# A decoder-layer step on one core: the late modulation steps write their transfers one place ahead of their matmuls

## The chip, the cores and the metric

One core of one Trainium2 chip runs the whole program. The metric is the device time of one execution in microseconds (us), as the median of several runs. Engines are named as the profile names them: PE (TensorE, the matmuls) and PEld (its weight loads), DVE (VectorE), ACT (ScalarE), POOL (GpSimd) and SP (SyncE, which here issues nearly all transfers; SPq is its queue).

## What is computed

One layer of a conditioned decoder in float32, for a 256-token prompt and for 8 sequences of 4 new tokens, so 288 columns in all. The conditioning vectors give six modulation vectors of 2048 values for each sequence; the rest is a gated-delta branch and a pooling branch that are merged, and then a feed-forward layer.

```python
mod = jax.nn.silu(c) @ w_ada + b_ada                       # w_ada: 2048 x 12288
sh1, sc1, gt1, sh2, sc2, gt2 = jnp.split(mod, 6, axis=-1)
u = ada_modulate(rms_norm(x, norm1_g), sh1, sc1)
mix, ... = token_mixers(u, ...)                            # u @ w_in, conv, delta rule, pooling, w_proj_a, w_proj_b, w_out
x = x + gt1[:, None, :] * mix
h = ada_modulate(rms_norm(x, norm2_g), sh2, sc2)
gate, up = jnp.split(h @ w_gate_up, 2, axis=-1)
x = x + gt2[:, None, :] * ((jax.nn.silu(gate) * up) @ w_down)
```

## The kernel before

**Weight chunks.** Every large product runs through `gemm` (L127 to L147). It takes a panel of 512 output columns and walks over its rows in chunks of 256 (`KB = 2` blocks of 128). For each chunk, `load_raw` (L114) has SP load a tile `raw` of 512 KB, ACT rounds each half into `wh` (L123), DVE (in a few panels POOL) subtracts to get the rest `wl` (L124), and PE does 24 matmuls of 128x288 (L141), six for each of the four output tiles `g0` to `g3`. There are `RAW = 7` tiles `raw` and `WH = 4` each of `wh` and `wl`, which are two chunks' worth. When a panel is done, `evac` empties `g0` to `g3`, in some panels with DVE's addition to `acc` (L435).

**Modulation steps.** The generator `ada` (L181 to L232) computes one modulation vector and gives control back after each step. Its late calls, the vectors `M_GT1`, `M_SC2`, `M_SH2` (the chain `later`) and `M_GT2` (`last_ada`), have `m == 16` and take 8 steps each. One step loads four tiles `raw` of 512 KB from `w_ada` and does 8 matmuls of 32x512 into `ada` (L218), which the profile records as 16. These four tiles come from the same seven `raw` tiles as the weight chunks, except the first two steps of `last_ada` (`ahead=2`), which load ahead into other tiles. After the last step the vector is turned round by PE (L225) and added up (L231).

**Where a step is written.** `gemm` calls `fill()` after each chunk; `Fill` adds `every` to a counter and resumes the generator each time the counter passes 1. `every` is 0.2 while `later` runs (one step in 5 chunks), and 0.085 for `last_ada` in the feed-forward layer (one in 11.8 chunks).

**What sets the order.** A scheduler that follows data, free tiles and priorities by its own clock puts what is written into one fixed order for each engine. `high_priority()` lets instructions go ahead; all matmuls of a step but the first have it. `issue_after(ins)` forbids that an instruction stands ahead of `ins` on its engine. Each engine then works strictly in its order, and SP too: a transfer that waits for a free `raw` tile holds back all transfers behind it.

Of the kernel before, what the change touches and what calls it, by code (L numbers as in the profile page):

```python
# [24 lines left out]
KB = 2  # L25
# [48 lines left out]
def tile_step(ctx: ExitStack, tc: tile.TileContext, at, t):  # L74
# [52 lines left out]
    def gemm(srcs_of, xs, evac, kbs, eng=vec, late=False):  # L127


        ps = [psg.tile([P, 512], F32, tag="g", name=f"g{j}") for j in range(4)]  # L130
        kbs = list(kbs)
        for c in range(0, len(kbs), KB):
            wh, wl = load_split(srcs_of(kbs[c]), eng)
            for j in range(4):
                o = ps[j][:, 0:N]
                last = c + KB == len(kbs)
                terms = [(w, x, i) for i in range(KB) for w, x in ((wh, 0), (wh, 1), (wl, 0))]
                if late and c == 0:
                    terms.sort(key=lambda v: v[1])
                for n, (w, x, i) in enumerate(terms):  # L140
                    mm = pe.matmul(o, w[i][:, j * P:(j + 1) * P], xs(kbs[c + i])[x], start=c + n == 0,  # L141
                                   stop=last and n == 3 * KB - 1)
                if last:
                    with tc.high_priority():
                        evac(j, o)
            fill()
        return mm  # L147

# [32 lines left out]
    def ada(*d0s, n=16, pool=None, ahead=0):  # L181


        m = n * len(d0s)
        w = m // 4 * P
        ps = psd.tile([P, 512], F32, tag="ada", name="ada")
        per = max(m // 8, 1)
        step = max(8 // m, 1)
        first = pool and d0s[0] == M_SH1
        pair = {4: 1 if first else 2, 8: 4, 16: 2}[m]  # L190

        def load(c, pool):
            loads = []
            for k in range(c, c + step * pair, step):
                raws = []
                for x in range(per):
                    if per > 1:
                        d = (d0s if len(d0s) > 1 else (d0s[0], d0s[0] + 8))[x]
                        srcs = [(t["w_ada"][0, k * P:(k + 1) * P, d * P:(d + 8) * P], 0, 1024)]
                    else:  # L200
                        srcs = [(t["w_ada"][0, k * P:(k + step) * P, d0 * P:(d0 + n) * P], i * n * P, (i + 1) * n * P)
                                for i, d0 in enumerate(d0s)]
                    raws.append(load_raw(srcs, qp if first and k >= 8 else pool, step))
                loads.append((k, raws))
            return loads

        early = {}
        for c in range(0, ahead * step * pair, step * pair):
            early[c] = load(c, pool or qp)
            yield  # L210
        for c in range(0, 16, step * pair):
            loads = early.get(c) or load(c, pool)

            todo = [(k, raws, i, j) for k, raws in reversed(loads) for i in range(step) for j in (2, 3, 0, 1)]
            for y, (k, raws, i, j) in enumerate(todo):
                x, q = divmod(j, 4 // per)
                with tc.high_priority() if y else nullcontext():
                    in_turn(pe.matmul(ps[32 * j:32 * j + 32, 0:w], cpad[:, k + i, :], raws[x][:, i, q * w:(q + 1) * w],  # L218
                                      start=c == 0 and y < 4, stop=c + step * pair == 16 and y + 4 >= len(todo)))
            if c + step * pair < 16:  # L220
                yield
        sb = wpool.tile([P, 512], F32, tag="adasb", name="adasb", bufs=1)
        act.copy(sb[:, 0:w], ps[:, 0:w])
        for i in range(0, w, P):
            pe.transpose(ps[:, i:i + P], sb[:, i:i + P], ident)  # L225
        pv = ps[:, 0:w].rearrange("p (b q m) -> p q b m", q=4, m=32)
        k = 4 // len(d0s)
        for i, d0 in enumerate(d0s):
            md = mod[:, d0:d0 + n, :].rearrange("p (q b) m -> p q b m", q=k)
            v = va[:, d0:d0 + n].rearrange("p (q b) -> p q b", q=k)  # L230
            vec.tensor_tensor(md, pv[:, i * k:(i + 1) * k, :, 0:9], bc(v, 3, [P, k, n // k, 9]), ALU.add)  # L231
        yield  # L232
# [8 lines left out]

    class Fill:

        gen, every, n = iter(()), 1.0, 0.0

        def __call__(self):
            self.n += self.every
# [4 lines left out]
    fill = Fill()  # L252
# [65 lines left out]
    with tc.tile_pool(name="st", bufs=1) as st:  # L318
# [44 lines left out]
        for i in range(3):  # L363
            n = xt[i].shape[0]
# [22 lines left out]
        for n, (k0, k1) in enumerate(STEPS):  # L387
            dn = k1 - k0
# [36 lines left out]

            more = n + 1 < len(STEPS)
            fill.gen = first_ada(*STEPS[n + 1], st) if more else later
            fill.every = 4 / (dn // KB * len(FIRST) - 5) if more else 0.2
            for p, c0 in enumerate(FIRST):
                def evac(j, ps, n=n, p=p):  # L430
                    a = acc[p][:, j, :]
                    if n == 0:
                        act.copy(a, ps)
                    else:
                        vec.tensor_tensor(a, a, ps, ALU.add)  # L435
# [601 lines left out]
        mm = gemm(cols_of(t["w_out"][0], 512 * p), xs_m, evac, range(16))  # L1037
    with tc.issue_after(mm.ins):
        next(last_ada)
    fill.every, fill.n = 0.085, 0  # L1040


    rn = cst.tile([P, 3], F32, name="rn")
# [144 lines left out]
```

## Time and profile before

| what | value |
|---|---|
| median of 3 runs | 1805.72 us (1804.52 to 1808.49) |
| the profiled execution | 1801.66 us |
| its span, first to last instruction | 1799.8 us |
| PE busy | 1749.2 us, 97% |
| PEld busy | 1651.6 us, 92% |
| DVE / ACT / POOL busy | 1001.3 / 751.0 / 234.0 us |
| bytes moved | 371.23 MB, mean 206 GB/s |

The profiled execution is 1.86 us longer than its span and 4.06 us shorter than the median. Matmuls overlap in the records, so 97% does not mean that PE works at its peak; what counts is where PE waits, and for whom.

### The profile page before, as it was taken

To read this page: it belongs to the slowest core of one execution; us is meant where nothing else is said; L and a number is where in the kernel's file an instruction comes from. 1 tells how busy PE (TensorE), PEld (TensorE's weight loads), DVE (VectorE), ACT (ScalarE), POOL (GpSimd) and SP (SyncE) were. 2 spreads that over 40 slices of the span, in tenths; PEclk is the share of its full clock that TensorE was granted. 3 is DMA by queue.
4 is the path that set the end of the run, shared out by engine and by line. 5 is a ranking of instruction groups with operands and counts; after the bars stand their busy time and mean duration, and the time that the engine had idled before them with its cause. 6 is when DMAs were issued, how large, how long until landed. Compare 5 with 4: busy or idle time off the path is not lost.

```text
span 1799.8 us, 37784 instructions
## 1 busy us (share of the span) xinstructions
PE 1749.2 (97%) x14772; PEld 1651.6 (92%) x14772; DVE 1001.3 (56%) x2101; ACT 751.0 (42%) x1534; POOL 234.0 (13%) x391
## 2 busy tenths in 40 slices
PE   5999998999999999999999999999999999999997
PEld 3979997888899898899989999999999999999997
DVE  2456569755666676764564444455445445544454
ACT  4523346542344333444444444444334444444333
POOL 1000015420222444211241000000000000000000
PEclk9999999999999999999999999999999999999999
DMA  9988756677577585885647667665555555555542
GB/s 292 316 300 304 234 169 202 213 229 246 187 252 234 189 268 177 271 294 179 218 150 234 211 205 224 188 203 165 164 165 164 168 167 169 154 175 164 162 156 87
DMA packets 227210, 371.23 MB, mean 206 GB/s; under 512 B 18335, under 2 KB 118168, under 8 KB 226608
## 3 DMA queue, kind: packets, MB, share of 16 engines
q1 hardware_dynamic: 223224, 357.02, 61.7%
q0 software_dynamic: 3808, 11.80, 2.1%
q8 instruction: 116, 1.90, 0.4%
q14 instruction: 62, 0.51, 0.1%
HBM read 361.16 MB, written 7.96 MB: 205 GB/s over the span
## 4 chain that ended last, share of the span: by engine, by line
PE 91%; DMA 4%; DVE 2%; issue 1%; ACT 0%; POOL 0%; SPq 0%; DVEq 0%; POOLq 0%; ACTq 0%
PE g L141 81%; PE ada L218 4%; DMA raw<-in_w_ada_dram 3%; DVE wl L124 1%; PE pks L726 1%; DVE cy L286 0%; DMA raw<-in_w_in_dram 0%; PE py L646 0%; PE pp L651 0%; PE pnr L545 0%; PE py L907 0%; DMA xt<-in_x_prompt_dram 0%; PE px L1011 0%; DMA pw<-in_pool_w_dram 0%; DMA dtb<-in_dt_bias_dram 0%
## 5 line engine op out<-in xcount | busy, mean ns | idle before, releaser
L141 PE MATMUL g<-rq,wh 128*128 128x288 f32 x7296 | 1443.2, 298 | 10.6 <-DVE acc L435 6.2
L141 PEld LDWEIGHTS g<-rq,wh 128*128 128x128 f32 x7296 | 1150.8, 188 | 37.2 <-issue 10.9
L141 PE MATMUL g<-rq,wl 128*128 128x288 f32 x3648 | 1014.3, 296 | 0.3 <-POOL wl L124 0.3
L124 DVE TENSOR_TENSOR wl<-raw,wh 128x512 fp32r<-128x512 f32 x910 | 611.7, 702 | 627.0 <-ACT wh L123 606.7
L123 ACT CAST wh<-raw 128x512 fp32r<-128x512 f32 x944 | 545.3, 618 | 821.7 <-PE g L141 742.5
L141 PEld LDWEIGHTS g<-rq,wl 128*128 128x128 f32 x3648 | 664.8, 188 | 4.3 <-issue 1.3
L218 PE MATMUL ada<-raw,cpad 128*32 128x512 f32 (+2 forms) x1152 | 98.5, 474 | 16.0 <-DMA raw<-in_w_ada_dram 16.0
L169 POOL TENSOR_TENSOR ro<-ro,cfix 128x1 f32<-128x1 f32 (+1 forms) x3 | 1.6, 559 | 838.0 <-DVE ro L1150 838.0
L218 PEld LDWEIGHTS ada<-raw,cpad 128*32 128x32 f32 x1152 | 32.9, 115 | 52.8 <-issue 38.1
L435 DVE TENSOR_TENSOR acc<-acc,g 128x288 f32<-128x288 f32 x144 | 61.0, 448 | 23.3 <-PE g L141 23.0
L124 POOL TENSOR_TENSOR wl<-raw,wh 128x512 fp32r<-128x512 f32 x34 | 45.8, 1367 | 51.6 <-ACT wh L123 50.4
L141 PE MATMUL g<-q,wh 128*128 128x288 f32 x256 | 49.4, 294 | 0.0
L286 DVE SCALAR_TENSOR_TENSOR cy<-xc,vb,cy 128x312 f32<-128x312 f32 x72 | 42.5, 610 | 5.6 <-ACT cy L284 4.7
L141 PEld LDWEIGHTS g<-q,wh 128*128 128x128 f32 x256 | 40.3, 189 | 0.0
L141 PE MATMUL g<-q,wl 128*128 128x288 f32 x128 | 35.2, 296 | 0.0
L1099 DVE SCALAR_TENSOR_TENSOR fgg<-fth,fgg 128x288 f32<-128x288 f32 x44 | 20.0, 455 | 14.0 <-ACT fgg L1098 14.0
L973 DVE SCALAR_TENSOR_TENSOR x<-g,mod,x 128x256 f32<-128x256 f32 x48 | 22.9, 478 | 7.0 <-PE g L141 5.9
L1097 ACT ACTIVATE fth<-g 128x288 f32<-128x288 f32 x44 | 18.3, 416 | 13.5 <-PE g L141 13.4
L141 PEld LDWEIGHTS g<-q,wl 128*128 128x128 f32 x128 | 23.2, 188 | 0.0
L659 POOL MEMSET T<- 32x64 f32 x8 | 1.1, 155 | 156.7 <-PE pab L444 148.4
L1104 DVE TENSOR_TENSOR fgg<-fgg,g 128x288 f32<-128x288 f32 x44 | 19.9, 451 | 2.7 <-PE g L141 0.4
L1098 ACT ACTIVATE fgg<-g 128x288 f32<-128x288 f32 x44 | 18.4, 417 | 0.0
(336 smaller groups left out, 976.2 us busy)
## 6 DMA issues: line engine op xcount, KB each, us to landing
raw<-in_w_gate_up_dram SPq DMA_DIRECT2D x352, 256.0 KB, 2.9
raw<-in_w_in_dram SPq DMA_DIRECT2D x144, 512.0 KB, 4.6
raw<-in_w_ada_dram SPq DMA_DIRECT2D x128, 512.0 KB, 5.6
raw<-in_w_down_dram SPq DMA_DIRECT2D x88, 512.0 KB, 4.0
raw<-in_w_ada_dram SPq DMA_DIRECT2D x128, 256.0 KB, 5.5
raw<-in_w_out_dram SPq DMA_DIRECT2D x32, 512.0 KB, 3.9
raw<-in_w_proj_b_dram SPq DMA_DIRECT2D x16, 512.0 KB, 4.5
raw<-in_w_proj_a_dram SPq DMA_DIRECT2D x16, 512.0 KB, 4.6
```

The costliest lines, as they stand in the source:

```text
L123: act.copy(wh[i], raw[:, i, :])
L124: eng.tensor_tensor(wl[i], raw[:, i, :], wh[i].bitcast(F32), ALU.subtract)
L141: mm = pe.matmul(o, w[i][:, j * P:(j + 1) * P], xs(kbs[c + i])[x], start=c + n == 0, stop=last and n == 3 * KB - 1)
L218: in_turn(pe.matmul(ps[32 * j:32 * j + 32, 0:w], cpad[:, k + i, :], raws[x][:, i, q * w:(q + 1) * w], start=c == 0 and y < 4, stop=c + ste ...
L286: vec.scalar_tensor_tensor(y[:, 0:L], xc[:, m:m + L], vb[:, 24 * m + no:24 * m + no + 1], y[:, 0:L], ALU.mult, ALU.add)
L435: vec.tensor_tensor(a, a, ps, ALU.add)
L726: pe.matmul(pks[NS * i:NS * i + NS, x * P:(x + 1) * P], km[i // 2][:, i % 2, b, :], S[i][:, b, :], start=b == 0, stop=b == NB - 1)
L973: vec.scalar_tensor_tensor(x[:, j, 0:NP], ps[:, 0:NP], mod[:, gate + d, 0:1], x[:, j, 0:NP], ALU.mult, ALU.add)
L1097: act.activation(th, ps, AF.Tanh, scale=0.5)
L1098: act.activation(gg, ps, AF.Copy, scale=0.5)
L1099: vec.scalar_tensor_tensor(gg, th, 1.0, gg, ALU.add, ALU.mult)
L1104: vec.tensor_tensor(gg, gg, ps, ALU.mult)
```

## The change

In a late step (`m == 16`) the four loads are now written at one place between chunks and the matmuls at the next: the generator gives control back between the two. The first matmul of such a step may not stand ahead of the last matmul of the newest chunk, which `gemm` notes in `fill.last`. Steps whose loads were already written ahead (`ahead`) stay as they were. Since a step now needs two calls, `every` is doubled, to 0.4 and 0.17, so that a vector takes as many chunks as before. The 0.3 during the last panel of `w_out` stays.

```diff
                     with tc.high_priority():
                         evac(j, o)
+            fill.last = mm
             fill()
         return mm
...
             loads = early.get(c) or load(c, pool)
+            tied = m == 16 and c not in early
+            if tied:
+                yield
...
-                with tc.high_priority() if y else nullcontext():
+                with tc.high_priority() if y else tc.issue_after(fill.last.ins) if tied else nullcontext():
                     in_turn(pe.matmul(ps[32 * j:32 * j + 32, 0:w], cpad[:, k + i, :], raws[x][:, i, q * w:(q + 1) * w],
...
-        gen, every, n = iter(()), 1.0, 0.0
+        gen, every, n, last = iter(()), 1.0, 0.0, None
...
-            fill.every = 4 / (dn // KB * len(FIRST) - 5) if more else 0.2
+            fill.every = 4 / (dn // KB * len(FIRST) - 5) if more else 0.4
...
-    fill.every, fill.n = 0.085, 0
+    fill.every, fill.n = 0.17, 0
```

The queue of SP around the 14th late step, in the pooling branch, of before. Each row is a transfer into a `raw` tile; the names in brackets are the counters that it waits for: `DVE_49` and `PE_49` stand for work of DVE (a subtraction L124 that frees a `raw` tile) and of PE (a matmul of a step that frees one), `DMAHW` for transfers done long before.

```order
L114 DMA raw_7018<-in_w_in_dram 128x2x512 [waits DMAHW2_49,DVE_49]
L114 DMA raw_7163<-in_w_in_dram 128x2x512 [waits DMAHW3_49,DVE_49]
L114 DMA raw_7197<-in_w_in_dram 128x2x512 [waits DMAHW4_49,DVE_49]
L114 DMA raw_7231<-in_w_in_dram 128x2x512 [waits DMAHW1_49,DVE_49]
L114 DMA raw_7265<-in_w_in_dram 128x2x512 [waits DMAHW5_49,DMAHW0_49,PE_49]
L114 DMA raw_7299<-in_w_ada_dram 128x1024 [waits DMAHW7_49,DMAHW6_49,PE_49]
L114 DMA raw_7301<-in_w_ada_dram 128x1024 [waits PE_49]
L114 DMA raw_7303<-in_w_ada_dram 128x1024 [waits DMAHW2_49,DVE_49]
L114 DMA raw_7305<-in_w_ada_dram 128x1024 [waits PE_49]
L114 DMA raw_7315<-in_w_in_dram 128x2x512 [waits DMAHW3_49,DVE_49]
L114 DMA raw_7349<-in_w_in_dram 128x2x512 [waits DMAHW1_49,PE_49]
```

The same place in the changed kernel:

```order
L114 DMA raw_7018<-in_w_in_dram 128x2x512 [waits DMAHW2_49,DVE_49]
L114 DMA raw_7163<-in_w_in_dram 128x2x512 [waits DMAHW7_49,DVE_49]
L114 DMA raw_7197<-in_w_in_dram 128x2x512 [waits DMAHW3_49,DMAHW0_49,DVE_49]
L114 DMA raw_7231<-in_w_ada_dram 128x1024 [waits DMAHW4_49,DMAHW1_49,DVE_49]
L114 DMA raw_7233<-in_w_ada_dram 128x1024 [waits DMAHW6_49,DMAHW5_49,PE_49]
L114 DMA raw_7235<-in_w_ada_dram 128x1024 [waits PE_49]
L114 DMA raw_7237<-in_w_ada_dram 128x1024 [waits PE_49]
L114 DMA raw_7239<-in_w_in_dram 128x2x512 [waits DMAHW2_49,DVE_49]
L114 DMA raw_7273<-in_w_in_dram 128x2x512 [waits PE_49]
L114 DMA raw_7315<-in_w_in_dram 128x2x512 [waits DMAHW3_49,DVE_49]
L114 DMA raw_7349<-in_w_in_dram 128x2x512 [waits DMAHW0_49,DVE_49]
```

The four loads of the step moved ahead of two weight chunks in SP's queue: before, five chunks from `raw_7018` to `raw_7265` stand ahead of them, now three, and the other two stand behind. In both, three of the four loads wait for matmuls of the step before (`PE_49`).

PE's order at the matmuls of the same step, of before (`ada` is the step, `g1` to `g3` are output tiles of the chunk in work):

```order
L141 MATMUL g2_7161<-rq_263,wh_7200 128x288
L141 MATMUL g2_7161<-rq_264,wh_7200 128x288
L141 MATMUL g2_7161<-rq_263,wl_7202 128x288
L218 MATMUL ada_6121<-raw_7305,cpad_82 32x512 x2
L218 MATMUL ada_6121<-raw_7303,cpad_82 32x512 x2
L218 MATMUL ada_6121<-raw_7301,cpad_82 32x512 x2
L218 MATMUL ada_6121<-raw_7299,cpad_82 32x512 x2
L141 MATMUL g3_7162<-rq_263,wh_7165 128x288
L141 MATMUL g3_7162<-rq_264,wh_7165 128x288
```

And of the changed kernel:

```order
L141 MATMUL g3_7162<-rq_1352,wh_7276 128x288
L141 MATMUL g3_7162<-rq_1353,wh_7276 128x288
L141 MATMUL g3_7162<-rq_1352,wl_7278 128x288
L222 MATMUL ada_6053<-raw_7237,cpad_82 32x512 x2
L222 MATMUL ada_6053<-raw_7235,cpad_82 32x512 x2
L222 MATMUL ada_6053<-raw_7233,cpad_82 32x512 x2
L222 MATMUL ada_6053<-raw_7231,cpad_82 32x512 x2
L141 MATMUL g0_7159<-rq_2170,wh_7317 128x288
L141 MATMUL g0_7159<-rq_2171,wh_7317 128x288
```

The step moved from inside a chunk (60 chunk matmuls behind the step before it) to behind the chunk `raw_7273`, five whole chunks behind the step before it; `raw_7239` and `raw_7273` are the fourth and the fifth of these chunks.

## Rows read from the trace of the kernel before

**Rows 1.** The page: span, busy time of PE, granted clock and GB/s in 40 slices.

```profile
span 1799.8 us, 37784 instructions
PE 1749.2 (97%) x14772; PEld 1651.6 (92%) x14772; DVE 1001.3 (56%) x2101; ACT 751.0 (42%) x1534; POOL 234.0 (13%) x391
PEclk9999999999999999999999999999999999999999
...
GB/s 292 316 300 304 234 169 202 213 229 246 187 252 234 189 268 177 271 294 179 218 150 234 211 205 224 188 203 165 164 165 164 168 167 169 154 175 164 162 156 87
```

**Rows 2.** Whom PE waited for, 240 to 1180 us: total us, times, longest us.

```profile
PE g L141 <- DVE acc L435: 5.8, 4, 4.4
PE g L141 <- ACT rq L1070: 2.3, 1, 2.3
PE pn L986 <- DVE sq L1025: 1.8, 1, 1.8
PE ada L218 <- DMA raw<-in_w_ada_dram: 1.2, 2, 0.8
...
PE g L141 <- POOL wl L124: 0.3, 1, 0.3
```

**Rows 3.** Instructions of L218, 240 to 1180 us, and what their idle time waited for.

```profile
L218 PE MATMUL ada<-raw,cpad x512: 592/592/617, 263.4 to 1167.7; 128*32 128x512 f32 x171
its engine sat idle before it (us, times) until:
  issue: 23.4, 90
  DMA raw<-in_w_ada_dram: 3.2, 5
```

**Rows 4.** The chain of waits, 770 to 800 us: start us, us, work.

```profile
778.25 1.85 PE ada L218 x16
780.10 12.97 PE g L141 x96
793.07 1.85 PE ada L218 x16
```

**Rows 5.** The chain of waits, 540 to 595 us.

```profile
547.28 1.85 PE ada L218 x16
549.13 3.39 PE g L141 x24
...
554.21 1.96 PE g L141 x14
...
556.28 3.01 PE g L141 x22
559.29 1.85 PE ada L218 x16
```

**Rows 6.** SP's queue, 545 to 566 us: first issue, length of the issues, how many.

```profile
548.77 1.94 SPq L114 DMA_DIRECT2D raw<-in_w_ada_dram  x4
555.08 7.15 SPq L114 DMA_DIRECT2D raw<-in_w_in_dram  x5
```

**Rows 7.** Stretches: us; busy PE, PEld, DVE, ACT, POOL; granted clock, DMA share, GB/s.

```profile
240.00:340.00 100.00, 93.23 (x691) 84.89 (x690) 82.91 (x189) 57.13 (x139) 47.99 (x89) 0.98 0.64 203
500.00:600.00 100.00, 99.92 (x900) 90.97 (x900) 60.84 (x141) 45.27 (x99) 19.15 (x44) 1.00 0.73 241
960.00:1180.00 220.00, 220.00 (x1661) 211.63 (x1658) 105.03 (x181) 93.13 (x181) 0.00 (x0) 1.00 0.68 213
551.00:558.00 7.00, 7.00 (x58) 7.00 (x57) 6.22 (x14) 4.55 (x14) 4.86 (x12) 1.00 1.01 377
563.00:570.00 7.00, 7.00 (x61) 6.84 (x60) 5.35 (x11) 2.96 (x7) 2.52 (x4) 1.00 1.05 393
```

**Rows 8.** Transfers, 240 to 820 us: count, KB each, median us to landing.

```profile
raw<-in_w_ada_dram SPq DMA_DIRECT2D x96, 512.0 KB, 6.1
raw<-in_w_in_dram SPq DMA_DIRECT2D x87, 512.0 KB, 4.6
```

**Rows 9.** The page's groups of the two halves of a split: busy us, mean ns.

```profile
L124 DVE TENSOR_TENSOR wl<-raw,wh 128x512 fp32r<-128x512 f32 x910 | 611.7, 702 | 627.0 <-ACT wh L123 606.7
L123 ACT CAST wh<-raw 128x512 fp32r<-128x512 f32 x944 | 545.3, 618 | 821.7 <-PE g L141 742.5
```

**Rows 10.** DVE in order of time, 278 to 285.5 us.

```profile
278.77 0.68 DVE L124 TENSOR_TENSOR wl<-raw,wh 128x512 fp32r<-128x512 f32 x1
279.37 1.50 DVE L896 SCALAR_TENSOR_TENSOR yp<-win,xp 128x256 f32<-128x256 f32 x1
...
284.09 1.53 DVE L435 TENSOR_TENSOR acc<-acc,g 128x288 f32<-128x288 f32 x4
```

## The prediction

> **What bounds the kernel now.** I read the page first: PE is busy 97% of the span, at the higher of its two clock levels (2.4 GHz) in every slice [rows 1]. Busy time of a pipelined engine hides small holes, so I went on to the list of waits, for the stretch in which the late steps run, 240 to 1180 us [rows 2]. There the reader is to see how little there is: the five rows come to 11.4 us, and the step's matmuls, which the change is about, waited for their own transfers 1.2 us, twice, at most 0.8 us. The view of L218 alone [rows 3] adds what the weight loads waited just ahead of a matmul, 3.2 us in 5 waits; its 23.4 us of "issue" are pauses of some 0.3 us inside the steps, which come with the small tiles and stay. The chain of waits then gives the pace that nothing can beat here: 96 chunk matmuls, four chunks, take 12.97 us, so 3.24 us a chunk, and a step 1.85 us [rows 4]. So the kernel is bound by PE issuing matmuls, and the change can win only what PE waits, or lose by making it wait. The granted clock is 0.98 from 240 to 340 us and 1.00 in the other stretches [rows 7]; none of my terms makes PE idle long enough to expect another level, and I price nothing for it.
>
> **The change part by part.** The sum is made on the profiled execution, 1801.66 us.
>
> 1. *Work.* 30 steps are tied: 3 vectors x 8, and 6 of the last vector. They issue the same 4 loads and 8 matmuls (16 records) at 1.85 us a step, and the doubled `every` gives the same one step in 5 and in 11.8 chunks. So 30 x 0 = 0 us.
>
> 2. *The waits that go.* In before, a step's loads and matmuls are written together, and the loads run only as far ahead as the scheduler's clock says. In the place shown in the order, the four loads are issued from 548.77 to 550.71 [rows 6] and the matmuls follow at 559.29, after 60 chunk matmuls, without a wait [rows 5]; in two other places it was just too late. Afterwards the loads are issued when the step before is done (they wait for its `raw` tiles) and are needed five chunks later, 5 x 3.24 = 16.2 us. Their median landing is 6.1 us [rows 8]. So the waits go: -1.2 us by [rows 2], with bounds of 0 and -3.2 us (all of the DMA row of [rows 3], if every bit of weight-load waiting was on the path). I take -1.2, since PE's own row is the nearest to what PE loses.
>
> 3. *What is queued behind the loads.* This is the price. SP is a strict queue, and two weight chunks per period now stand behind four step loads. The step holds four of seven `raw` tiles for its whole period, where it held them for some two or three chunks. Which chunk gets late? The fourth after a step: PE has three chunks in hand, 3 x 3.24 = 9.7 us after the step's last matmul. Its transfer: three step loads go out as the old step's matmuls free their tiles; the first of them some 0.85 us before the step ends, as in [rows 5, 6] (there the step runs from 547.28 for 1.85 us, the second transfer that its matmuls free goes out at 548.77, and one follows the other by 1.94 / 4 = 0.48 us). Four transfers of 0.524 MB at the 385 GB/s of the two packed stretches [rows 7] take 5.4 us; a lone transfer's 4.6 us [rows 8] less its own 1.4 us of moving leaves up to 3.2 us before the first byte counts. So it lands about -0.85 + 3.2 + 5.4 = 7.8 us after the step at the worst of these prices, and 6.7 us (0.6 + 6.1) by the step loads' own median. Then ACT needs 0.62 us and DVE 0.70 us [rows 9]: ready at 8.0 to 9.1 us of 9.7. The cover holds by 0.6 to 1.7 us in the stretches that have nothing but chunks, and by more where side work of the branches stands between. I take 0 us. If the cover is gone, each us costs one at up to 23 places (24 steps of the first three vectors less one). An end on the other side is excluded: nothing in this part makes a chunk earlier than PE wants it.
>
>     The rows show 377 and 393 GB/s over 7 us with the queue full [rows 7]. The Trainium skill, "DMA: Bandwidth & Descriptors", section "Where 436 GB/s comes from", says that the memory side gives one core about 358 GB/s. By that figure (an estimate) the four transfers take 5.9 us, not 5.4, and the cover shrinks by 0.5 us. The trace disagrees, and the measurement decides.
>
> 4. *The last vector's steps.* In the feed-forward layer the loads go out about 6 chunks before the matmuls, so weight chunks live on three `raw` tiles for 6 chunks in 12. Three tiles give a chunk three periods, 9.7 us, from the split that frees its tile to its own split; landing 4.6 us and the split 2 x 0.62 + 0.70 us fit. 0 us; DVE and ACT have room there (105 and 93 of 220 us [rows 7]). A gain is bounded by the one wait of part 2 that lies there and is counted already.
>
> 5. *Everything else that moves.* From 240 to 340 us DVE is the tight engine: 82.91 of 100 us busy, PE 93.23 [rows 7]. PE's longest wait, 4.4 us, is for four additions of a panel's end that stand behind 5 us of convolution and pooling work in DVE's order [rows 2, 10]. The change writes the steps elsewhere in this stretch, so DVE's order and the place where PE can use a step as a filler change. The total of DVE's work does not. Bounds: -5.8 us (the waits for L435 all go) and +3 us (the first steps, 1.85 us each, no longer fill a hole; one and a half of them). I take 0, since DVE's sum bounds this stretch and is the same.
>
> Sum: 0 - 1.2 + 0 + 0 + 0 = -1.2 us, so 1800.5 us for the profiled execution; against the median of 1805.72, which is 4.06 above it, **1804.5 us**.
>
> **The rivals.** The limit between "same" and the others is 0.2%, 3.6 us, about what a measurement of this kernel can tell from no change.
>
> *The fourth chunk comes late (slower).* One mechanism: `raw` tiles. If it lands more than 9.7 - 1.3 = 8.4 us after the step's end, PE stops in every period. For it: at the 316 GB/s of the page's densest slice [rows 1] four transfers take 6.6 us and not 5.4, and the chunk lands at -0.85 + 3.2 + 6.6 = 9.0 us, 0.6 us late; ACT and DVE may also have other work ahead of the split. The 24 steps of before lie (793.07 - 263.4) / 23 = 23.0 us apart [rows 3, 4], while five chunks and a step take 18.1 us, so side work helps at some; I take 15 of the 23 places as bare: 15 x 0.6 = 9.0 us, 1804.5 + 9.0 = 1813.5 us. Against it: that slice is at the program's start, and within the stretch the full queue moved 377 and more. It decides from 8.4 us on, and would show as the same hole once a period.
>
> The Trainium skill, "Perfetto Trace Analysis", section "Optimization Strategy", reads a hole that repeats on the busiest engine as a sign that there is not enough room for the next tile. By that rule the change, which keeps four of seven tiles longer, moves towards such holes. The trace of before shows none [rows 2], so it neither bears the rule out nor speaks against it.
>
> *The tight DVE stretch untangles (faster).* If the new order puts the panel additions ahead of the pooling work, part 5 gives up to -5.8 us: 1804.5 - 5.8 = 1798.7 us. For it: the wait is an accident of order, 4.4 us in one place. Against it: DVE has 83 us of work in 100.
>
> *The loads can't go ahead.* They are written earlier but wait for `PE_49`, the step before, so that nothing moves on the chip: 1805.7 us. Against it: two chunks fewer stand ahead of them in SP's order. Its time lies within "same".
>
> **How the numbers follow.** My forecast, with the last rival (same): 0.47, of which 0.12 for that rival. DVE untangles, or more of [rows 3] goes than I count (faster by over 0.2%): 0.27. The fourth chunk is late, or DVE's stretch gets worse (slower by over 0.2%): 0.26. The likeliest case is 1804.5, with its own range of 1802.1 to 1809.3. To hold 8 in 10, the range goes to the faster rival's 1798.7 and a little below it, for part 2's other bound (-2.0 us): 1797; above, to the late chunk at 1813.5: 1814.
>
> **What would show it.** In the changed kernel's list of waits, 240 to 1180 us: the row of L218 for its transfers gone or under 0.3 us (part 2); no row of L141 for `wh`, `wl` or a weight transfer above 1 us in sum (part 3). If part 3 is wrong, PE or PEld waits for ACT's L123 or DVE's L124 at the fourth chunk behind each step, 10 to 25 times with some 0.6 us. In the chain of waits four pure chunks should still take 12.97 us and a step 1.85 us (part 1). From 240 to 340 us PE should be busy 92 to 95 us; above 97 would be the faster rival, below 90 the slower side of part 5. The forecast is wrong if PE's waits for L435 change by over 3 us, or if a chunk lands later than 8.4 us behind a step.

## The result, and the profile of the changed kernel

The changed kernel takes 1818.61 us (median of 4 runs, 1815.3 to 1820.67), the kernel before 1805.12 us (1801.71 to 1808.49 beside it): a ratio of 1.0079, 95% interval 1.0064 to 1.0094, so 13.5 us slower. The forecast was 1804.5 us, 1797 to 1814. The profiled executions lie as far apart: 1815.3 us (span 1813.5) against 1801.66 us (span 1799.8).

The page of the changed kernel, to be held against [rows 1]: span, busy time of PE, granted clock in 40 slices.

```profile
span 1813.5 us, 37767 instructions
PE 1761.0 (97%) x14772; PEld 1660.4 (92%) x14772; DVE 999.2 (55%) x2101; ACT 752.0 (41%) x1534; POOL 229.2 (13%) x391
PEclk9999998999999999999989999999999999999999
```

PE has the same 14772 matmuls and is busy 11.8 us longer: a part of the time was spent in matmuls at the lower of the two clock levels. The page shows it in the slice from 272 us and in the one from 907 to 952 us (digit 8). The list of waits (whom PE waited for: total us, times, longest us), 240 to 1200 us, answers to [rows 2]:

```profile
PE pot L818 <- DVE oo L815: 5.3, 1, 5.3
PE g L141 <- DVE acc L439: 5.2, 4, 2.7
PE g L141 <- ACT rq L1074: 2.3, 1, 2.3
PE pn L990 <- DVE sq L1029: 1.9, 1, 1.9
PE g L141 <- ACT wh L123: 0.7, 1, 0.7
PE px L750 <- issue: 0.5, 1, 0.5
```

The step's own row (L218, now L222) is gone, as forecast. Two rows that matter are new: 5.3 us for `oo`, once, and 0.7 us for a chunk's `wh`. Smaller rows of before are gone, so the whole list comes to 16.1 us, against 13.5 us for the same stretch before. (Lines from 146 on count 1 to 4 more than before: L170 is L169, L439 is L435, L1074 is L1070, L818 is L814.) Followed through the trace, PE reaches the `pn` matmuls of the norm at 930.54 us (920.28 before, +10.3), the first chunk of the feed-forward layer at 940.37 (927.38, +13.0); behind that 0.7 us more is lost.

**The place at 654 to 660 us.** PE in order of time (start us, us, work, in brackets the idle time ahead and what ended it), then GpSimd, both of the changed kernel:

```profile
654.13 0.29 PE L141 MATMUL g<-rq,wh 128*128 128x288 f32 x1
659.71 0.66 PE L818 MATMUL pot<-cfix,oo 128*128 128x128 f32 x2 [5.28 <-DVE oo L815]
```

```profile
647.47 0.95 POOL L791 DMA_DIRECT2D out_dram<-sst  x1 [1.52 <-DVE sst L789]
655.88 0.89 POOL L941 DMA_DIRECT2D sst<-in_state_delta_dram  x1 [7.46 <-DMA out_dram<-sst]
656.78 0.72 POOL L170 TENSOR_TENSOR m<-m,cfix 128x2 f32<-128x2 f32 x1
```

And GpSimd of the kernel before at the same work:

```profile
646.16 0.92 POOL L787 DMA_DIRECT2D out_dram<-sst  x1 [0.38 <-DVE m L810]
648.41 0.73 POOL L169 TENSOR_TENSOR m<-m,cfix 128x2 f32<-128x2 f32 x1 [1.33 <-DVE m L808]
649.12 1.29 POOL L780 TENSOR_TENSOR wx<-wr,cm 96x512 fp32r<-96x512 f32 x1
651.17 0.95 POOL L937 DMA_DIRECT2D sst<-in_state_delta_dram  x1 [0.77 <-DMA out_dram<-sst]
```

The delta-rule state `sst` is written out and its buffer then reloaded for the second group of heads; the reload must wait until the write-out has landed. Both are issued in GpSimd's order of instructions. Before, the small power (`m`, L169, the inverse root that scales a head's output) stands ahead of the reload. Now it stands behind it, and so behind 7.46 us of waiting; `oo` waits for `m`, and PE's `pot` for `oo`. The change touches none of these lines: it only shifted the scheduler's clock.

**The clock.** Stretches (us; busy PE, PEld, DVE, ACT, POOL; granted clock, DMA share, GB/s) of the changed kernel:

```profile
240.00:340.00 100.00, 94.76 (x696) 88.53 (x696) 81.04 (x183) 56.95 (x139) 45.30 (x87) 0.95 0.60 196
655.00:665.00 10.00, 5.29 (x32) 5.32 (x33) 6.15 (x11) 1.14 (x2) 4.33 (x6) 0.83 0.84 270
925.50:945.50 20.00, 15.86 (x88) 11.06 (x87) 12.28 (x32) 7.20 (x19) 8.87 (x13) 0.67 0.18 53
```

and of the kernel before around the same pauses at `pn` and `rq`:

```profile
915.50:935.50 20.00, 15.86 (x115) 12.62 (x114) 14.19 (x35) 9.54 (x24) 11.60 (x16) 0.91 0.17 54
```

In the last pair PE is busy for the same 15.86 of 20 us and waits the same (1.85 and 2.3 us), but gets 88 matmuls done where it got 115: the granted clock averages 0.67 and 0.91. Between 200 and 1200 us the low stretches, all at half (1.2 of 2.4 GHz), are in the changed kernel's profile 273.4 to 276.8, 287.1 to 293.9, 659.1 to 662.5 and 932.2 to 945.8 us, and before 285.5 to 288.9 and 927.2 to 930.6 us. All of them begin at or near a pause of PE.

What pauses and clock come to is read over the whole stretch, in the same columns: before, before again (g4), changed, changed again (e2).

```profile
200.00:1200.00 1000.00, 985.19 (x8692) 911.67 (x8691) 609.11 (x1341) 429.83 (x918) 226.62 (x372) 1.00 0.67 216
200.00:1200.00 1000.00, 986.22 (x8673) 911.25 (x8672) 606.99 (x1337) 428.65 (x916) 226.64 (x372) 0.99 0.67 216
200.00:1200.00 1000.00, 982.64 (x8599) 906.22 (x8599) 599.56 (x1327) 424.18 (x904) 221.85 (x372) 0.99 0.66 215
200.00:1200.00 1000.00, 979.65 (x8568) 903.26 (x8567) 598.79 (x1325) 423.56 (x903) 219.97 (x372) 0.99 0.66 213
```

PE is idle for what is missing to 1000 us: 14.8, 13.8, 17.4 and 20.3 us. The half clock lasts 6.8, 13.7, 27.3 and 27.3 us, and by an estimate half of that time is lost. The two sums account for the spans. Changed against before: 2.6 us more idle time and 10.2 us of clock, for a span 13.7 us longer. The second profiles, which lie near the medians of their kernels: 6.6 and 6.8 us, for 13.2 us. Against the first profile of before the same sum fits 16 of the other 19 profiles to about 2 us and is 3 to 7 us off in f4, h4 and i1. So the waits are only a part of the loss. Nor is the clock all chance: its mean over all executions is 0.9913 for the kernel before (101 of them, 0.988 to 0.995; its first profile, at 0.995, lies at the top), 0.9878 for the four of the changed kernel and 0.9895 for the six of e2. Times the span, that is an estimate of some 3 to 6 of the 13.5 us.

### The profile page after: what moved, and what is told of

It reads as the page before. It is cut to its first block, busy times and chain, and to the rows that moved or that the text cites. A ratio compares the mean times of both kernels' runs of the same rounds, so it can differ in the third digit from the quotient of the medians.

```text
span 1813.5 us, 37767 instructions
## 1 busy us (share of the span) xinstructions
PE 1761.0 (97%) x14772; PEld 1660.4 (92%) x14772; DVE 999.2 (55%) x2101; ACT 752.0 (41%) x1534; POOL 229.2 (13%) x391
## 4 chain that ended last, share of the span: by engine, by line
PE 55%; DVE 2%; DMA 1%; ACT 0%; SPq 0%; issue 0%; DVEq 0%; ACTq 0%
PE g L141 53%; PE ada L222 1%; DVE rq L1075 1%; DMA raw<-in_w_proj_a_dram 0%; DVE hp L1073 0%; DMA raw<-in_w_gate_up_dram 0%; PE px L1015 0%; PE pf L1132 0%; PE pn L990 0%; DVE wl L124 0%; ACT jf L1135 0%; DVE xo L1162 0%; PE plc L831 0%; SPq L114 0%; DVE x L977 0%; DVE sq L1029 0%
## 5 line engine op out<-in xcount | busy, mean ns | idle before, releaser
L124 DVE TENSOR_TENSOR wl<-raw,wh 128x512 fp32r<-128x512 f32 x910 | 608.6, 699 | 629.0 <-ACT wh L123 616.0
L123 ACT CAST wh<-raw 128x512 fp32r<-128x512 f32 x944 | 545.6, 618 | 846.8 <-PE g L141 736.6
L222 PE MATMUL ada<-raw,cpad 128*32 128x512 f32 (+2 forms) x1152 | 100.7, 482 | 14.9 <-DMA raw<-in_w_ada_dram 14.9
L170 POOL TENSOR_TENSOR ro<-ro,cfix 128x1 f32<-128x1 f32 (+1 forms) x3 | 1.6, 557 | 836.1 <-DVE ro L1154 836.1
L222 PEld LDWEIGHTS ada<-raw,cpad 128*32 128x32 f32 x1152 | 33.6, 116 | 52.3 <-issue 38.6
L439 DVE TENSOR_TENSOR acc<-acc,g 128x288 f32<-128x288 f32 x144 | 61.0, 449 | 21.5 <-PE g L141 21.2
L124 POOL TENSOR_TENSOR wl<-raw,wh 128x512 fp32r<-128x512 f32 x34 | 46.1, 1377 | 58.2 <-ACT wh L123 57.0
```

Source lines behind the costliest of these rows:

```text
L123: act.copy(wh[i], raw[:, i, :])
L124: eng.tensor_tensor(wl[i], raw[:, i, :], wh[i].bitcast(F32), ALU.subtract)
```

## The experiments

Three theories to begin with. **Q**: GpSimd's row costs what is lost. **R**: weight chunks come late because steps hold `raw` tiles (the prediction's own rival). **C**: the granted clock differs by chance between executions. Later came **O**: the kernel before is a good draw among orders, and any shift of the late steps costs several small waits. Its rivals **M** and **W** say that what the change does costs the rest by itself; **T** (tiles) and **D** (a crowd of transfers) are two readings of R.

Two readings are used for all runs, both from 240 to 1200 us: what PE waited for a chunk's ACT copy or difference (`wh` L123, `wl` L124), and what ACT's L123 waited for chunk transfers. The first counts short waits too that the lists leave out (up to 0.3 us in all). "Tiles held" is worked out from issue times and steps: for the 24 steps of the first three vectors, the sum over their loads of (start of the step's last matmul minus issue of the load), divided by the time from the first step to the last one's last matmul.

| run | ratio to before | 95% interval | PE for late chunks, us | ACT for chunk transfers, us (times) | tiles held |
|---|---|---|---|---|---|
| before, first profile | 1 | | 0.5 | 5.9 (2) | 3.3 of 7 |
| before, again (g4) | 1.0001 | 0.9992 to 1.0009 | 0.5 | 14.3 (5) | 3.3 |
| changed | 1.0079 | 1.0064 to 1.0094 | 0.9 | 42.0 (17) | 4.4 |
| changed, again (e2) | 1.0072 | 1.0051 to 1.0093 | 2.6 | 43.4 (16) | 4.3 |
| e1, GpSimd row moved | 1.0044 | 1.0027 to 1.0061 | 2.9 | 58.4 (21) | 4.3 |
| e3, loads ahead alone | 1.0045 | 1.0028 to 1.0061 | 0.3 | 21.8 (8) | 3.7 |
| e4, ordering alone | 1.0053 | 1.0036 to 1.0070 | 0.4 | 6.4 (2) | 4.0 |
| f3, ordering, row moved | 1.0028 | 1.0019 to 1.0038 | 0.2 | 9.0 (3) | 4.0 |
| f4, last vector alone | 1.0012 | 1.0003 to 1.0021 | 1.6 | 4.2 (2) | 3.3 |
| f1, before shifted 0.2 | 1.0079 | 1.0066 to 1.0093 | 0.1 | 5.3 (2) | 3.5 |
| f2, before shifted 0.8 | 1.0037 | 1.0025 to 1.0049 | 3.0 | 6.4 (3) | 3.6 |
| h4, before shifted 0.6 | 0.9991 | 0.9982 to 1.0000 | 0.0 | 5.8 (3) | 3.4 |
| g1, changed, reloads late | 1.0065 | 1.0051 to 1.0078 | 3.8 | 57.0 (20) | 4.3 |
| g2, before, reloads late | 1.0014 | 1.0005 to 1.0022 | 0.3 | 11.8 (4) | 3.3 |
| g3, f1 with reloads late | 1.0017 | 1.0008 to 1.0026 | 0.0 | 11.7 (6) | 3.5 |
| h1, changed, shifted 0.2 | 1.0173 | 1.0155 to 1.0191 | 7.8 | 103.5 (30) | 4.7 |
| h2, changed, shifted 0.5 | 1.0021 | 1.0011 to 1.0030 | 3.4 | 36.9 (14) | 4.3 |
| h3, changed, shifted 0.8 | 1.0048 | 1.0036 to 1.0060 | 2.4 | 42.4 (19) | 4.3 |
| i1, changed, six tiles | 1.0192 | 1.0171 to 1.0212 | 17.3 | 145.0 (51) | 4.1 of 6 |
| i2, before, six tiles | 0.9995 | 0.9986 to 1.0005 | 0.7 | 8.7 (3) | 3.2 of 6 |

### GpSimd's row: e1 and e2

`rsqrt_small` returns its instruction, `chunk` keeps it in `pows`, and one reload is ordered behind it:

```diff
-            dmg(out=s_t, in_=t["state_delta"][0, :, 4 * g + i].rearrange("b k v -> k b v"))
+            with tc.issue_after(pows[1, 0, 0].ins) if (g, i) == (1, 2) else nullcontext():
+                dmg(out=s_t, in_=t["state_delta"][0, :, 4 * g + i].rearrange("b k v -> k b v"))
```

In the instruction order one row moves on GpSimd, one on DVE and one on PE; ACT and SP are as they were.

> The changed kernel with one row moved on three engines: the third state load of the second group on GpSimd is ordered behind the pow of the chunk m1_7658, so that the pow no longer waits for that load (and for the write-out of the old state ahead of it). Theory Q (GpSimd's queue): the 5.28 us wait of PE for L815's oo goes, and with it the half-clock stretch behind it (659.1 to 662.5, 3.4 us at half speed = 1.7 us): 7 us of the 13.5 us come back, ratio to the kernel before 1.0036 to 1.0045. Theory R (weight chunks late for want of raw tiles): nothing changes, 1.0079. Theory C (chance of the granted clock): nothing beyond 2 us, 1.007 to 1.009.

> The changed kernel once more, for a second profile. Theory Q: the wait for oo at 654 to 660 us is there again with 5 to 5.5 us, since it is in the order. Theory C: the half-clock stretch of 932 to 946 us (13.6 us, against 3.4 us at the same place of the kernel before) is another length or gone, and the time differs by what it gives back, up to 5 us. If both the wait and the long stretch come again, the stretch too belongs to the change.

e1: 1811.93 us, against 1816.65 us of the unaltered changed kernel (e2) on the same chip: 1.0044 and 1.0072, 4.7 us apart. In e1 GpSimd goes on, and the reload waits alone:

```profile
644.70 0.94 POOL L793 DMA_DIRECT2D out_dram<-sst  x1 [1.52 <-DVE sst L791]
646.98 0.72 POOL L170 TENSOR_TENSOR m<-m,cfix 128x2 f32<-128x2 f32 x1 [1.34 <-DVE m L814]
651.44 0.92 POOL L944 DMA_DIRECT2D sst<-in_state_delta_dram  x1 [3.74 <-DMA out_dram<-sst]
```

PE's row for `oo` is gone, and its busy time from 650 to 660 us is 10.00 of 10 at clock 1.00. So Q holds: 1.0044 lies in its range, though against e2 it is some 5 us and not 7, and with so few executions the 95% interval of that difference is 0 to 10 us; f3 and g3 below repeat it. In the second profile of the changed kernel (e2) the same wait was only 2.54 us; the write-out took 6.1 us there and 8.1 us in the first. The order makes the trap, and the time of the write-out sets its price. The low clock behind it came again (659.1 to 662.5 us). For the pauses at `pn` and `rq`, 20 us each of e1, e2 and f1 (below), in the columns of above:

```profile
918.00:938.00 20.00, 15.86 (x114) 12.62 (x113) 14.86 (x37) 8.75 (x22) 11.29 (x16) 0.91 0.19 56
925.00:945.00 20.00, 15.85 (x94) 11.05 (x93) 11.69 (x31) 6.28 (x17) 9.72 (x14) 0.76 0.18 58
928.00:948.00 20.00, 15.86 (x87) 11.06 (x86) 11.79 (x30) 5.89 (x16) 8.82 (x13) 0.66 0.17 53
```

The same work and the same pauses, and the granted clock is 0.91, 0.76 and 0.66; the second profile of the kernel before (g4) has 0.74 there. So C is true of this place: its 3 us in the first pair of profiles are a draw of the execution, not the change. But the medians differ by 13.5 us, and the mean clock differs too, so C is not the explanation of the whole.

### The two halves: e3, e4 and f3

e3 leaves the loads ahead and takes out the ordering; e4 takes out the loads ahead (and the doubled spacing) and keeps the ordering; f3 is e4 with the edit of e1.

```diff
e3
-                with tc.high_priority() if y else tc.issue_after(fill.last.ins) if tied else nullcontext():
+                with tc.high_priority() if y else nullcontext():
e4
-            if tied:
-                yield
...
-            fill.every = 4 / (dn // KB * len(FIRST) - 5) if more else 0.4
+            fill.every = 4 / (dn // KB * len(FIRST) - 5) if more else 0.2
...
-    fill.every, fill.n = 0.17, 0
+    fill.every, fill.n = 0.085, 0
```

> One half of the change alone: the step's loads are written one place ahead of its matmuls, but the first matmul is not ordered behind the newest chunk. In the instruction order GpSimd's pow of the first chunk stands ahead of the second state load, as in the kernel before. Theory Q: no wait for oo above 1 us, ratio 0.997 to 1.002. Theory R: the four raw tiles are held as long as in the changed kernel, so the loss stays, 1.005 to 1.009, with holes of PE at wh or wl behind the steps. Theory C: between 0.998 and 1.004.

> The other half alone: loads and matmuls at one place again (every 0.2 and 0.085), only the step's first matmul ordered behind the newest chunk. GpSimd's order has the pow behind the third state load, as in the changed kernel. Theory Q: PE waits for oo about 5 us at 650 to 670 us and the ratio is 1.003 to 1.008. Theory R: the tiles are held as in the kernel before or shorter, so 1.000, at most 1.002 for step loads that come late. Theory C: between 0.998 and 1.004.

> The half with the ordering alone, and in it the third state load of the second group ordered behind GpSimd's pow, as it was done in the changed kernel. Theory Q: the 5.83 us wait of PE for oo goes, and 2.8 us that its half-clock stretch took: 1.0053 becomes 1.000 to 1.002. If GpSimd's row is not what that wait costs: 1.004 to 1.006. Theory O would keep a rest of 0.002 to 0.004.

e4, 1.0053: the wait for `oo` is there (5.8 us), as Q said, with no load ahead. Moving the row (f3) takes it out: 1.0028, so 4.5 us of the 6 to 9.5 that Q expected, with a rest as O had it. e3, 1.0045: no wait for `oo`, but not free as Q said, and nor are the late chunks R spoke of there (0.3 us). Its list of waits has other ones: a step for its own transfer (2.75 us at 752 us), `pw` (2.5 us) and `xr` (2.0 us). The first two are loads that stand behind other loads in SP's queue; `xr` is loaded by GpSimd. So without the trap each half alone costs something (1.0045 and 1.0028), as the two together do (1.0044), and that brought theory O.

### Is it the order? f1, f2, h4 and f4

f1, f2 and h4 are the kernel before with one line, the start of the count that spaces the late steps (0.2, 0.8, 0.6); f4 is the change for the last vector alone.

```diff
             fill.every = 4 / (dn // KB * len(FIRST) - 5) if more else 0.2
+            fill.n = fill.n if more else 0.2
```

> The kernel before with nothing but the count that spaces the late steps started at 0.2 instead of 0: no load ahead, no ordering behind a chunk, the same work; every step of the first three vectors only falls one chunk earlier or so. GpSimd's two pows of the first chunks stand ahead of the second state load. Theory O (the kernel before is a good draw among orders, and any other order of these steps costs several small waits of 1 to 2 us): ratio 1.002 to 1.006, with a new set of small waits of PE between 240 and 960 us. Rival M (the loss that is left without GpSimd's wait, 1.0044 in the run with that wait removed, comes from what the change does: loads ahead or the ordering): 0.999 to 1.001.

> As the run before, with the count started at 0.8. Both pows stand ahead of the second state load here too. Theory O: 1.002 to 1.006, with other places of the small waits. Rival M: 0.999 to 1.001.

> The kernel before with the count started at 0.6, nothing else. Pows ahead of the second and the third state load. Theory O: like f1 and f2, 1.002 to 1.008, hardly below 1.001, as the kernel before is the best of its draws. Theory W: as theory O, since nothing of the change is in it; if it gave 1.000, two of four draws without the change would be free, and the kernel before no rare draw.

> The change for the last vector alone (its six steps in the feed-forward layer: loads at one place, matmuls at the next, ordered behind the newest chunk); the first three vectors as in the kernel before, so that the order is the same as there up to some 800 us. All theories: no difference, 0.999 to 1.001, and no wait of PE over 0.7 us between 960 and 1200 us. If part of the rest of 8 us sits in the feed-forward layer, it shows here as 1.002 or more.

A shift of the steps, with nothing of the change, gives 1.0079, 1.0037 and 0.9991, where M had 0.999 to 1.001 for the first two. f1 loses as much as the change does, and the largest part in the same trap with another victim, the fourth reload and the decay `lt` behind it. GpSimd and then PE:

```profile
666.50 0.93 POOL L788 DMA_DIRECT2D out_dram<-sst  x1
...
676.18 0.93 POOL L938 DMA_DIRECT2D sst<-in_state_delta_dram  x1 [7.64 <-DMA out_dram<-sst]
677.17 0.44 POOL L615 TENSOR_TENSOR lt<-lt,cm 128x128 f32<-128x128 f32 x1
```

```profile
672.78 0.31 PE L647 MATMUL py<-Tc,mt 32*32 32x32 f32 x16
679.30 0.33 PE L647 MATMUL py<-Tc,mt 32*32 32x32 f32 x8 [6.22 <-DVE Tc L642]
```

f2 has it too: PE waits 2.84 us for a `wl` that stands in DVE's order behind `mt`, which needs the same `lt`. h4 draws none of it. So O holds in part: a shift may cost as much as the change, or nothing; the kernel before is one of two free draws among four. f4 gives 1.0012: the last vector's share is some 2 us, in a wait of 0.75 and one of 0.56 us for a late chunk at 952 us, where I had taken 0.

### The reloads moved out of the way: g1, g2, g3, and g4

All four reloads of the second group are written in `chunk` behind the last GpSimd products (`TTc`) of the three chunks at work, and ordered behind them:

```diff
+        if smp and g == 1:
+            for k in ((1, 1, 0), (1, 1, 2), (1, 2, 0)):
+                ties.enter_context(tc.issue_after(last_tt[k].ins))
+            S = load_state(1)
+            ties.close()
```

> The changed kernel with all four state reloads of the second group written behind the last GpSimd products of the chunks at work (so that on GpSimd nothing which PE needs soon stands behind a reload that waits for a write-out). Theory Q (the reload in GpSimd's queue): no wait of PE for oo above 0.5 us at 640 to 690 us, ratio 1.002 to 1.005, as in the run where one row was moved (1.0044). If the reloads now come too late for the sample chunk: a new wait of PE at pks, and 1.006 or more. Theory O (the rest belongs to the order in other places): it stays above 1.002.

> The kernel before with the same move of the four reloads. PE waits there for none of them (POOL idles 2.3 us at most for a write-out, and no row of PE shows it), so theories Q and O both expect 0.999 to 1.002; a gain over 0.002 would say that the reloads cost the kernel before something too.

> The kernel before with the count of the late steps started at 0.2 (1.0079, with 6.2 us of PE waiting at 673 to 679 us: DVE waits for GpSimd's lt, which stands behind the fourth reload, which waits 7.6 us for the write-out), now with the four reloads moved. Theory Q: that wait and the half-clock stretch behind it go, 6.2 + 3 us, ratio 1.002 to 1.004. If the wait has another cause it stays at 1.006 or more.

> The kernel before once more, for a second profile: the half-clock stretches between 200 and 1200 us (6.8 us in the first profile: 285.5 to 288.9 and 927.2 to 930.6). Theory C (where a pause of PE meets a lower clock is chance): other lengths, 3 to 17 us, at the same pauses. Time 0.999 to 1.001.

g3: the shifted kernel goes from 1.0079 to 1.0017, some 11 us, and no PE wait of 0.4 us is left between 640 and 690 us. That shows the trap a second time, in a kernel without the change. g2, 1.0014: nothing to gain in the kernel before, as expected. g1: the wait for `oo` is gone, but the time is 1.0065 and not 1.002 to 1.005. Its four reloads now go out together from 668.9 us on and share the DMA engines with step and chunk loads; ACT waits 5.94 us for a chunk's transfer (until 687.06 us), DVE's order stands behind that chunk, and PE waits 2.6 us for `Yc` at 688 us, with low clock from 688.1 to 695.0 us. One wait was exchanged for another, which is a lead to R.

### The changed kernel in other orders: h1, h2, h3

The same one-line shift, in the changed kernel (0.2, 0.5, 0.8).

> The changed kernel with the count of the late steps started at 0.2 (the steps fall half a chunk to one chunk earlier). GpSimd's pows stand ahead of the second state load. Theory O (the loss is the draw of the order): anywhere between 1.000 and 1.008, other than 1.0079, with its own list of waits. Theory W (what the change does costs about 1.0044 by itself): 1.0035 to 1.008, never below.

> The changed kernel with the count started at 0.5. Pows ahead of the second state load. Theory O: 1.000 to 1.008, waits at other places than in h1. Theory W: 1.0035 to 1.008.

> The changed kernel with the count started at 0.8. Pows ahead of the second state load, but the reloads follow one another closely. Theory O: 1.000 to 1.008. Theory W: 1.0035 to 1.008.

1.0173, 1.0021 and 1.0048, none with the trap. The worst, h1, left the range of both theories on the upper side, and h2 left W's on the lower. h1's largest row is R's, and the view of ACT's L123 shows the same in all seven-tile runs with the whole change (group, tile, count; busy us, mean ns; idle us and what ended most of it), here before, changed and h1:

```profile
L123 ACT CAST wh<-raw 128x512 fp32r<-128x512 f32 x479 | 277.7, 618 | 398.6 <-PE g L141 333.7 <-issue 46.5 <-ACT wh L123 5.5
```

```profile
L123 ACT CAST wh<-raw 128x512 fp32r<-128x512 f32 x472 | 273.9, 618 | 419.8 <-PE g L141 326.3 <-issue 32.9 <-DMA raw<-in_w_in_dram 21.7
```

```profile
L123 ACT CAST wh<-raw 128x512 fp32r<-128x512 f32 x459 | 265.6, 617 | 402.0 <-PE g L141 265.5 <-DMA raw<-in_w_in_dram 60.1 <-DMA raw<-in_w_proj_b_dram 19.7
```

Before, ACT waits nearly always for PE to free a `wh` tile: chunks are there in advance. In these runs PE is still the larger part (326.3 and 265.5 us above), but 14 to 30 times ACT waits for the transfer itself.

### Fewer raw tiles: i1 and i2

```diff
-RAW, WH = 7, 4
+RAW, WH = 6, 4
```

> The changed kernel with six raw tiles in place of seven. Theory T (tiles): with 4.3 held by the steps fewer than two are left for chunks, PE's waits for ACT's wh and DVE's wl between 240 and 1200 us grow from 0.9 to 2.9 us (three profiles) to 10 us and more, in most periods, and the ratio is 1.012 or more. Theory D (the crowd of transfers, not the tiles): those waits stay at 1 to 8 us and the ratio between 1.002 and 1.010, as in the draws of the order.

> The kernel before with six raw tiles in place of seven. Theory T: 3.3 of 6 are held, 2.7 left, as in the changed kernel with seven: PE's waits for wh and wl are 1 to 5 us (0.45 with seven) and the ratio 1.001 to 1.008. Theory D: at most 0.5 us, and a ratio that only the order draws, 0.999 to 1.008.

i1: 1.0192, and PE's waits for `wh` become the largest of its list, 240 to 1200 us:

```profile
PE g L141 <- ACT wh L123: 15.4, 11, 3.0
```

That is what T had expected (10 us and more, 1.012 or more) and D had not, in the changed kernel. It is one order, though, and h1 shows that an order alone can come near it. i2 went against T: with 3.2 of 6 held the kernel before loses nothing (0.9995, 0.7 us of late chunks). Both fit one series of single profiles, the tiles that are left for chunks: 3.3 and more (before and its shifts, e3) go with 0 to 0.5 us of late chunks (apart from f2's 2.84 us, which are the trap's, and f4's wait, which is the last vector's); 3.0 (e4, f3) with 0.2 to 0.4; 2.8 (i2) with 0.7; 2.65 to 2.75 (changed, e1, g1, h2, h3) with 0.9 to 3.8; 2.3 (h1) with 7.8; 1.9 (i1) with 17.3. In this series the edge lies just under three tiles, and the change moves the kernel from 3.7 to 2.65.

## Why the prediction was wrong

**Part 1, work.** Right. The step still takes 1.85 us, and 67 matmuls of pure chunk 8.92 us, the pace of before.

**Part 2, the waits that go.** Right. The steps no longer wait for transfers: PE's row is gone, and of L222's idle time in front of weight loads 0.6 us is left in 2 waits (3.2 in 5 before, [rows 3]).

**Part 3, raw tiles.** The mechanism was right and was even sized well; the decision at the edge was wrong. The chain of waits of the changed kernel passes through it at one step (start us, us, what):

```profile
792.45 1.92 PE ada L222 x16
...
794.86 6.74 DMA raw<-in_w_proj_a_dram
...
801.70 0.63 ACT wh L123
...
802.35 0.69 DVE wl L124
803.04 0.38 DVE ga L963
...
803.56 6.59 PE g L141 x48
```

The load is issued when the step's last matmul has freed its tile (794.37 us), lands 7.2 us behind the step and is split at 8.7 us: the prediction had 6.7 to 7.8 and 8.0 to 9.1. PE went on at 9.2 us, 0.16 us late, behind an addition that stood between in DVE's order, where I had counted 9.7 and a cover of 0.6 to 1.7 us. Two terms were mis-sized. The step holds more than the four tiles that I gave it, 4.35 on average, as the next step's first loads go out before the old step ends. And the kernel before did not hold them for "some two or three chunks": its first load stands a median of 19.5 us ahead of the step's end, six chunks, and 3.3 tiles were held on average; so the change adds one tile. The rival took 15 places at 0.6 us each, 9.0 us; the runs with the whole change and seven tiles show 1 to 10 places and 0.9 to 7.8 us in all. "An end on the other side is excluded" stood.

The prediction set beside this rival a rule of the Trainium skill, "Perfetto Trace Analysis", section "Optimization Strategy": holes that repeat on the busiest engine can mean that there is not enough room for the next tile. Here the trace of before had no such hole and the changed one has hardly any; the lack of room showed first on ACT, which went from 5.9 to 42.0 us of waiting for transfers while PE still waited under 1 us. By the rule one would have looked at PE alone and seen it late.

**Part 4, the last vector.** Taken at 0; f4 measured 1.0012 (1.0003 to 1.0021), some 2 us. A late chunk between 952 and 982 us is in six of the seven profiles with the whole change and seven tiles (0.4 to 1.6 us), so the three tiles did not cover it there.

**Part 5, everything else that moves.** This is the step that failed. It looked at DVE from 240 to 340 us alone and let the rest of the order stand. There PE was busy 94.8 us, inside the 92 to 95 forecast, and the waits for L439 are 5.2 us (5.8 before), though in two pieces in place of one, with more low clock behind them (10.2 us against 3.4 in the first pair; e1, with the same order there, has 3.4). But the change also moved rows on GpSimd, 400 us further on, and one of them went behind a transfer that waits for another transfer, which cost some 5 us (e1, f3). That was in the instruction order of both kernels before any run, and no term or rival of the prediction names GpSimd's queue at all.

**The clock.** "At the higher of its two clock levels (2.4 GHz) in every slice" was a misreading: a 9 in that row means 90% or more. The trace of before itself has 3.4 us of half clock behind the 4.4 us pause at 280 us and 3.4 us behind the pauses around 925 us. Pauses of 1.9 to 6.2 us are mostly followed by half clock in these runs, and a term that makes PE wait has to carry that on top. The prediction priced nothing for it; by the estimate above it is 3 to 6 of the 13.5 us.

**The sum, in the order of what is shown.** Of 13.5 us, 5 us are GpSimd's row with the low clock behind it (e1 against e2; e4 against f3 gives 4.5). Late chunks are 0.9 to 2.9 us of PE's waits in the three profiles with the changed kernel's steps, besides what the clock adds. The rest, some 6 to 8 us, is not settled. By the count of idle time and half clock it is in good part lower clock, and for the remainder small waits at places that each order draws anew; no run takes the two apart. Over four orders each, setting f1's trap aside by g3 and the changed kernel's by e1, the kernel before gives 1.0000, 0.9991, 1.0037 and 1.0017, the changed one 1.0044, 1.0173, 1.0021 and 1.0048. The 1.0037 (f2) still has its own trap in it. The ranges overlap, the changed kernels lie higher; four draws do not say by how much. None of the variants beats the kernel before by more than a measurement can tell (h4, 0.9991).

## What to carry to other kernels

On every engine that both computes and issues transfers, look for a transfer that must wait for another transfer, and for what an edit may put behind it: the edit need not touch either line, since a scheduler's clock moves them. Loads that go ahead are paid in tiles, and the spare is read on the engine that fills the tiles (what ACT waits for), not on the bound one, which shows it only when it is used up. Before looking for causes, add up the bound engine's idle time and its time at the lower clock: here the two gave the 13 us between the profiles within 1 us, where the list of waits of the first pair showed 2.6 us. And with a kernel this full, shift the order once or twice without the change before crediting or blaming the change: here that alone gave -0.1% to +0.8%.

## What the runs showed of the hardware

The granted clock falls to half (1.2 GHz) at most PE pauses of some 2 to 6 us in this kernel (not at all: 2.9 us at 271 us of i2 has none behind it), and comes back while PE works; but the same pauses around 930 us come with 3.4 to 13.7 us of half clock in different executions (clock 0.91, 0.76, 0.74, 0.67, 0.66 over 20 us with the same busy time). A single profile cannot credit that to a change.

PE may also have waited for its own code. In the stretch of small matmuls around 600 us the profile names no releaser ("issue"); here e1 and e2:

```profile
602.07 0.40 PE L752 MATMUL px<-bb,TTc 32*32 32x128 f32 x3 [1.30 <-issue]
```

```profile
606.22 0.40 PE L750 MATMUL px<-bb,TTc 32*32 32x128 f32 x3 [1.55 <-issue]
```

In thirteen such waits near 600 or 696 us, in as many profiles (0.35 to 2.7 us), PE went on 1.26 to 1.52 us after a 16 KB packet of the instruction queue had landed, at times when that queue shares the DMA engines with weight loads (for e1 at 99.3% of their time). An execution has 116 such packets, one in some 15 us. That is a coincidence in time, thirteen times, and no experiment on it was made. The Trainium skill, "Runtime: NRT & Kernel Launch", section "Instruction fetch mechanics", says that an engine's code is refilled in 16 KB blocks and that this is mostly hidden; the packets' size agrees, and in this stretch it would not be hidden.
